# Reciprocal square roots on VectorE by a bit guess and Newton steps, in place of GpSimd's power, in a one-core encoder step

## The chip, the core and the metric

The kernel runs on one core of a Trainium2 chip. The metric is the device time of one execution in microseconds (us). The engines of the core are TensorE (PE, with its weight loads as PEld), VectorE (DVE), ScalarE (ACT), GpSimd (POOL) and SyncE (SP), whose queue issues nearly all DMA transfers. Each engine works through its own list of instructions in order; semaphores make one wait for another.

## The reference

One layer of a streaming encoder works on 1024 prompt tokens and 32 sample tokens with 1024 channels. The layer normalises its input, projects it to queries, keys, values and gates, runs three branches (windowed attention, a short convolution, attention into 256 memory tokens), gates and merges them, projects the result and adds the input; a last normalisation follows. What the change concerns is the normalisation, which occurs three times: of the input, of the memory tokens and of the output.

```python
def rmsnorm(x, g):
    x32 = x.astype(jnp.float32)
    y = x32 * lax.rsqrt(jnp.mean(x32 * x32, axis=-1, keepdims=True) + EPS)
    return (y * g.astype(jnp.float32)).astype(x.dtype)

# in reference(), cut:
q, k, v, ga, bb, cc, hh, gb, xq, gx, mg = split_inputs(xp, norm_g[l], w_in[l])   # rmsnorm(x, g) @ w
mk, mv = memory_kv(mem_prompt, mem_norm_g[l], w_mk[l], w_mv[l])                   # rmsnorm(mem, g) @ wk, wv
xp = xp + merge_branches(attn, ga, conv, bb, gb, xattn, gx, mg, w_pa[l], w_pb[l], w_px[l], w_out[l])
y_prompt = rmsnorm(xp, final_g)
y_sample = rmsnorm(xs, final_g)
```

## The kernel before

Channels lie on the partitions and tokens along the free axis; the 1056 tokens are held as two halves (the index `c`, 528 tokens each). Most products are done with numbers split into a high and a low part, three matmuls for one (`mm3`, L99 to L101), and the large input projections with a seven-product scheme on sums and differences of blocks. A framework puts the instructions of each engine into an order of its own before the program is built, from estimates of when operands are ready; so an edit in one function can move other instructions on the same engines, and on others.

The normalisation is done in these steps. ScalarE squares the eight pieces of a half (`x_squares`, L457) and VectorE adds the squares (`sq`, L461). `column_rstd` sums over the partitions with tiny matmuls against a column of ones (`cs...`, L417), so that tokens come to lie on partitions; VectorE scales the sum and adds epsilon (`va...`, L421); and GpSimd raises it to the power -0.5 (`rs...`, L424). `spread` (L428) multiplies the root with the identity on TensorE so that it stands along the free axis on all partitions (`rp...`), ScalarE copies that to `R...` (L436), and `x_norm` (L466) multiplies the eight pieces by it on VectorE. `x_blocks` and `x_sums` then split them into `xh` and `xl`.

At the start the first half has its root under the name `rsx` (88 partitions x 6 columns), the memory tokens theirs as `rsm` (128 x 2) and the second half again as `rsx`. Between them TensorE forms the memory keys `mkp` (`mk_step`, L585, four steps of eight products, each with 2 records in the trace). `mem_spread` (L557) spreads `rsm` to `rpm` and ScalarE copies it to `rm` (L563); `mk_out` multiplies `mkp` by `rm` (`mko`, L591) on VectorE, and the rest of it splits that into `mkh` and `mkl`. The first large products are those for keys and values (`pdkv`, `kv_group`), from the weights `whkv` and `wlkv`. The spreads and `pdkv` share two accumulation buffers (`bank2`), so the second `pdkv` waits until the copy has read the spread.

At the end `finish` (L1088) does the same for the output in four parts, under the name `rso` (88 x 3): two while output products (`wo`) for the second half of the tokens run, one a little later, and the last when nothing else is left.

Of the kernel before, what the change touches and what calls it, by code (L numbers as in the profile page):

```python
# [6 lines left out]
F32 = mybir.dt.float32  # L7
F32R = mybir.dt.float32r
AF = mybir.ActivationFunctionType
ALU = mybir.AluOpType  # L10
# [23 lines left out]
def stream_kernel(tc, A, O):  # L34
    nc = tc.nc
    act, dve, pool, pe, sp = nc.scalar, nc.vector, nc.gpsimd, nc.tensor, nc.sync

    from contextlib import ExitStack
    with ExitStack() as ctx:
        sb = ctx.enter_context(tc.tile_pool(name="sb", bufs=1))  # L40
        sm = ctx.enter_context(tc.tile_pool(name="sm", bufs=2))
# [28 lines left out]
        def bank2(name, i=None):  # L70

            if i is None:
                i = turns[0] = 1 - turns[0]
            return pp.tile([128, 2, 512], F32, name=name, tag=f"P{i}")

        def bank(name, shape=(128, 512)):
            return pq.tile(list(shape), F32, name=name, tag="Q")
# [13 lines left out]
        nhalf = cst[:, C_HALF:C_HALF + 1]  # L91
# [320 lines left out]
        def column_rstd(parts, cols, w, nm, pair_=False):  # L412

            ps = bank2(f"cs{nm}")[:, 0] if pair_ else bank(f"cs{nm}")
            for j in range(cols):
                for i, a in enumerate(parts):
                    pe.matmul(ps[:w, 2 * j:2 * j + 2], a[:, j * w:(j + 1) * w], one.broadcast_to([128, 2]),  # L417
                              start=i == 0, stop=i == len(parts) - 1)
            va = sm.tile([128, 6], F32, name=f"va{nm}", tag="va")
            pv_ = ps[:w, :2 * cols].rearrange("p (j t) -> p j t", t=2)  # L420
            dve.tensor_scalar(out=va[:w, :cols].unsqueeze(2), in0=pv_[:, :, 0:1], scalar1=1.0 / D, scalar2=EPS,  # L421
                              op0=ALU.mult, op1=ALU.add)
            rs = sm.tile([128, 6], F32, name=f"rs{nm}", tag="rs", bufs=3)
            pool.tensor_tensor(out=rs[:w, :cols], in0=va[:w, :cols], in1=nhalf[:w].broadcast_to([w, cols]), op=ALU.pow)  # L424
            return rs

        def spread(out, rs, j, w):
# [480 lines left out]
        for i in range(4):  # L908
            mem_scale(i)
            for k in (2 * i, 2 * i + 1):  # L910
                mv_step(k, wmv[k])
        sq = [x_squares(c) for c in range(2)]
        r0 = column_rstd([sq[0]], 6, 88, "x0", True)
        MS["rs"] = column_rstd([MS["acc"][:, :256], MS["acc"][:, 256:]], 2, 128, "m", True)
        mk_step(0)
        R0 = r_chunk(r0, "x0")
        x_norm(0, R0)
        mk_step(1)
        r1 = column_rstd([sq[1]], 6, 88, "x1", True)
        x_blocks(0, [xslot(slot(0, T4, l), f"b12{l}", F32R) for l in range(2)])  # L920
        kv = kv_group("kv", (T_K, T_V))
# [294 lines left out]
```

## Time and profile before

| what | value |
|---|---|
| median of 3 runs | 1005.92 us (1005.43 to 1006.57) |
| the profiled execution, its own time | 1011.11 us |
| its span, from the first to the last instruction | 1009.3 us |
| TensorE busy | 982.1 us, 97% of the span |
| VectorE busy | 510.7 us, 51%, 836 instructions |
| GpSimd busy | 561.4 us, 56%, 422 instructions |
| power operations on GpSimd (L424) | 7: two `rsx` (1.788 and 10.310 us), one `rsm` (1.023 us), four `rso` (0.852 to 1.296 us) |

Durations are taken from the one profiled execution, which is some 5 us longer than the median; a difference is carried over. An engine's idle time matters only where TensorE, the busiest, waits because of it.

### The profile page before, as it was taken

Reading aid. Unit: us, or ns where it says so; the run is one execution under the profiler, and the core shown is the slowest. Engines: PE = TensorE matmul, PEld = TensorE weight load, DVE = VectorE, ACT = ScalarE, POOL = GpSimd, SP = SyncE. Lnnn points to the kernel's source line nnn. Section 1 sums busy time; section 2 is a strip of 40 time slices with the busy share of each in tenths; the row PEclk is TensorE's granted clock in tenths of the full one; section 3 lists DMA queues with packets and bytes.
Section 4 is the critical chain, followed back from the end, with each engine's and each line's share of the span. In section 5 each row is a group of like instructions: output and inputs, shape, how many; then the busy total and the mean of one; then the engine's idle time right before and its main releaser. Section 6 shows DMA issues by size and latency. Waiting matters only on the chain.

```text
span 1009.3 us, 20193 instructions
## 1 busy us (share of the span) xinstructions
PE 982.1 (97%) x7887; PEld 958.1 (95%) x7887; DVE 510.7 (51%) x836; ACT 465.1 (46%) x969; POOL 561.4 (56%) x422
## 2 busy tenths in 40 slices
PE   8799999999999999999999999999999999999996
PEld 4699999999999999999999999999999999999996
DVE  3787333466575656565443333333374472552464
ACT  5454434455445454454454545545372242243452
POOL 0505677665667676767555555555554444444463
PEclk9899999999999999999999999999999999999998
DMA  9445633454423232322354444434686678653473
GB/s 338 145 150 156 204 133 110 152 170 138 128 67 103 74 112 85 99 75 86 105 161 149 154 151 148 138 120 153 210 281 201 182 201 254 183 188 88 126 233 118
DMA packets 115711, 153.06 MB, mean 152 GB/s; under 512 B 14400, under 2 KB 73888, under 8 KB 115616
## 3 DMA queue, kind: packets, MB, share of 16 engines
q1 hardware_dynamic: 115040, 151.24, 48.0%
q8 instruction: 62, 1.02, 0.4%
q10 hardware_dynamic: 576, 0.54, 0.2%
q14 instruction: 33, 0.27, 0.1%
HBM read 109.49 MB, written 42.25 MB: 150 GB/s over the span
## 4 chain that ended last, share of the span: by engine, by line
PE 85%; DVE 8%; DMA 2%; ACT 2%; POOL 2%; issue 1%; SPq 0%; POOLq 0%; DVEq 0%; ACTq 0%
PE y L99 4%; PE y L101 4%; PE y L100 4%; PE wo L99 3%; PE wo L101 3%; PE wo L100 3%; PE pamg L99 2%; PE pamg L100 2%; PE pdmg L99 2%; PE pamg L101 2%; PE pdmg L100 2%; PE pdmg L101 2%; PE pcmg L99 2%; PE pcmg L100 2%; PE pcmg L101 2%; PE mvp L550 2%
## 5 line engine op out<-in xcount | busy, mean ns | idle before, releaser
L95 POOL TENSOR_TENSOR wlp<-rp,whp 128x512 fp32r<-128x512 f32 x80 | 104.9, 1312 | 128.7 <-ACT whp L115 128.6
L115 ACT CAST whp<-rp 128x512 fp32r<-128x512 f32 x96 | 59.6, 621 | 130.3 <-PE y L100 78.7
L99 PE MATMUL y<-br,whp 128*128 128x264 f32 x384 | 109.2, 284 | 1.2 <-DVE z L271 1.2
L100 PE MATMUL y<-br,whp 128*128 128x264 f32 x384 | 109.1, 284 | 0.0
L101 PE MATMUL y<-br,wlp 128*128 128x264 f32 x384 | 109.0, 284 | 0.0
L95 POOL TENSOR_TENSOR wlmg<-S_mg,whmg 128x512 fp32r<-128x512 f32 x48 | 62.7, 1307 | 56.2 <-ACT whmg L115 42.5
L95 POOL TENSOR_TENSOR wlmg<-rmg,whmg 128x512 fp32r<-128x512 f32 x36 | 47.0, 1306 | 62.1 <-ACT whmg L115 59.3
L101 PE MATMUL wo<-zo,wlp 128*128 128x264 f32 x256 | 73.0, 285 | 0.8 <-POOL wlp L95 0.8
L99 PE MATMUL wo<-zo,whp 128*128 128x264 f32 x256 | 73.2, 286 | 0.3 <-ACT whp L115 0.3
L99 PEld LDWEIGHTS y<-br,whp 128*128 128x128 f32 x384 | 72.1, 188 | 1.3 <-ACT whp L115 1.3
L100 PE MATMUL wo<-zo,whp 128*128 128x264 f32 x256 | 72.6, 284 | 0.0
L100 PEld LDWEIGHTS y<-br,whp 128*128 128x128 f32 x384 | 72.3, 188 | 0.0
L101 PEld LDWEIGHTS y<-br,wlp 128*128 128x128 f32 x384 | 72.3, 188 | 0.0
L99 PE MATMUL pcmg<-xh,whmg 128*128 128x264 f32 x192 | 55.5, 289 | 1.2 <-DVE omg L218 1.2
L99 PE MATMUL pamg<-xh,whmg 128*128 128x264 f32 x192 | 55.3, 288 | 0.0
L99 PE MATMUL pdmg<-xh,whmg 128*128 128x264 f32 x192 | 55.2, 287 | 0.0
L100 PE MATMUL pcmg<-xl,whmg 128*128 128x264 f32 x192 | 54.7, 285 | 0.0
L100 PE MATMUL pdmg<-xl,whmg 128*128 128x264 f32 x192 | 54.7, 285 | 0.0
L100 PE MATMUL pamg<-xl,whmg 128*128 128x264 f32 x192 | 54.7, 285 | 0.0
L101 PE MATMUL pdmg<-xh,wlmg 128*128 128x264 f32 x192 | 54.6, 284 | 0.0
L101 PE MATMUL pcmg<-xh,wlmg 128*128 128x264 f32 x192 | 54.4, 284 | 0.0
L101 PE MATMUL pamg<-xh,wlmg 128*128 128x264 f32 x192 | 54.4, 283 | 0.0
(493 smaller groups left out, 3674.3 us busy)
## 6 DMA issues: line engine op xcount, KB each, us to landing
MGd<-omg SPq DMA_DIRECT2D x24, 528.0 KB, 3.6
sg<-MGd SPq DMA_DIRECT2D x48, 264.0 KB, 3.1
rmg<-in_w_in SPq DMA_DIRECT2D x48, 256.0 KB, 2.8
rp<-in_w_p SPq DMA_DIRECT2D x48, 256.0 KB, 3.1
rp<-in_w_out SPq DMA_DIRECT2D x48, 256.0 KB, 2.8
xr<-in_xT SPq DMA_DIRECT2D x8, 528.0 KB, 7.9
res<-in_xT SPq DMA_DIRECT2D x8, 528.0 KB, 5.7
qtw<-Qd SPq DMA_DIRECT2D x32, 128.0 KB, 2.6
```

Source lines behind the costliest of these rows:

```text
L95: eng.tensor_tensor(out=lo, in0=x, in1=hi.bitcast(F32), op=ALU.subtract)
L99: pe.matmul(out, lh, rh, start=first, stop=False, skip_group_check=free)
L100: pe.matmul(out, lh, rl, start=False, stop=False, skip_group_check=free)
L101: pe.matmul(out, ll, rh, start=False, stop=last, skip_group_check=free)
L115: act.copy(hi, src)
L550: pe.matmul(mps[m], mt(k)[:, m * 128:(m + 1) * 128], w, start=k == 0, stop=k == 7)
```

## The change

`column_rstd` computes the reciprocal square root on VectorE. The bits of the value `v` are read as an integer, shifted right by one, and subtracted from a constant, which gives a first guess `y` with the bits of a float; three Newton steps y <- y (1.5 - 0.5 v y y) follow. Each root is thus eleven instructions on VectorE, each working on the result of the one before, and GpSimd has no part in it. The function is called seven times: 77 instructions come and 7 go.

```diff
             rs = sm.tile([128, 6], F32, name=f"rs{nm}", tag="rs", bufs=3)
-            pool.tensor_tensor(out=rs[:w, :cols], in0=va[:w, :cols], in1=nhalf[:w].broadcast_to([w, cols]), op=ALU.pow)
+            t = sm.tile([128, 6], F32, name=f"rt{nm}", tag="rt", bufs=3)
+            v, y, t = va[:w, :cols], rs[:w, :cols], t[:w, :cols]
+            I32 = mybir.dt.int32
+            dve.tensor_scalar(out=t.bitcast(I32), in0=v.bitcast(I32), scalar1=1, scalar2=None, op0=ALU.logical_shift_right)
+            dve.tensor_scalar(out=y.bitcast(I32), in0=t.bitcast(I32), scalar1=-1.0, scalar2=float(0x5f3759df), op0=ALU.mult,
+                              op1=ALU.add)
+            for i in range(3):
+                dve.tensor_tensor(out=t, in0=y, in1=y, op=ALU.mult)
+                dve.scalar_tensor_tensor(out=t, in0=t, scalar=-0.5, in1=v, op0=ALU.mult, op1=ALU.mult)
+                dve.scalar_tensor_tensor(out=y, in0=t, scalar=1.5, in1=y, op0=ALU.add, op1=ALU.mult)
             return rs
```

The framework's order changes with it, in roughly the first tenth of the program and near its end; in between the order of every engine stays as it was. Lines behind the edit have numbers larger by nine in the changed kernel (L461 becomes L470, L585 becomes L594). In the new kernel L427 and L428 are the two integer instructions and L431 to L433 the Newton steps.

VectorE, from the first `vax` on, before (`sq` are the sums of squares of the second half, `xr` the input being normalised):

```order
L421 TENSOR_SCALAR vax_242<-csx_235 88x6
L421 TENSOR_SCALAR vam<-csm 128x2
L461 TENSOR_TENSOR sq_0_212<-sq_0_212,sq_2_217 128x528
L461 TENSOR_TENSOR sq_0_212<-sq_0_212,sq_3_220 128x528
L461 TENSOR_TENSOR sq_0_212<-sq_0_212,sq_4_223 128x528
L466 SCALAR_TENSOR_TENSOR xr_0_104<-xr_0_104,cst,Rx_271 128x528
L461 TENSOR_TENSOR sq_0_212<-sq_0_212,sq_5_226 128x528
L466 SCALAR_TENSOR_TENSOR xr_0_104<-xr_0_104,cst,Rx_271 128x528
```

The same place after the change:

```order
L421 TENSOR_SCALAR vax_242<-csx_235 88x6
L421 TENSOR_SCALAR vam<-csm 128x2
L427 TENSOR_SCALAR rtx_245<-vax_242 88x6
L470 TENSOR_TENSOR sq_0_212<-sq_0_212,sq_2_217 128x528
L428 TENSOR_SCALAR rsx_244<-rtx_245 88x6
L427 TENSOR_SCALAR rtm<-vam 128x2
L470 TENSOR_TENSOR sq_0_212<-sq_0_212,sq_3_220 128x528
L431 TENSOR_TENSOR rtx_245<-rsx_244 88x6
L428 TENSOR_SCALAR rsm<-rtm 128x2
L470 TENSOR_TENSOR sq_0_212<-sq_0_212,sq_4_223 128x528
L432 SCALAR_TENSOR_TENSOR rtx_245<-rtx_245,vax_242 88x6
L431 TENSOR_TENSOR rtm<-rsm 128x2
```

It goes on like this up to the addition of `sq_7`: all six additions now stand among the steps of the two chains, and the first multiplication of `xr` stands behind both chains.

VectorE at the second `rsx`, after the change (the last six steps of the chain; `xl` are low parts of the first half, `mko` and `mkl` the memory keys):

```order
L433 SCALAR_TENSOR_TENSOR rsx_320<-rtx_321,rsx_320 88x6
L95 TENSOR_TENSOR xl_5_340<-xr_2_114,xh_5_339 128x528
L431 TENSOR_TENSOR rtx_321<-rsx_320 88x6
L95 TENSOR_TENSOR xl_2_338<-xr_3_120,xh_2_337 128x528
L432 SCALAR_TENSOR_TENSOR rtx_321<-rtx_321,vax_318 88x6
L95 TENSOR_TENSOR xl_5_340<-xr_3_120,xh_5_339 128x528
L433 SCALAR_TENSOR_TENSOR rsx_320<-rtx_321,rsx_320 88x6
L600 TENSOR_TENSOR mko_396<-mkp_277,rm 128x512
L431 TENSOR_TENSOR rtx_321<-rsx_320 88x6
L600 TENSOR_TENSOR mko_405<-mkp_357,rm 128x512
L432 SCALAR_TENSOR_TENSOR rtx_321<-rtx_321,vax_318 88x6
L95 TENSOR_TENSOR mkl_400<-mko_396,mkh_399 128x512
```

One row follows that belongs to the chain, its last step (L433). Before the change `mko` stood behind the normalisation of the second half, well after this place.

TensorE at the end of `mkp`, before:

```order
L585 MATMUL mkp_324<-memt_116,rmk_150 128x256 x2
L428 MATMUL rpx_341<-cst,rsx_298 128x88 x6
L428 MATMUL rpm<-cst,rsm 128x128 x2
L99 MATMUL pdkv_407<-xh_0_302,whkv_383 128x264
L100 MATMUL pdkv_407<-xl_0_303,whkv_383 128x264
```

And after the change:

```order
L594 MATMUL mkp_357<-memt_116,rmk_150 128x256 x2
L437 MATMUL rpm<-cst,rsm 128x128 x2
L99 MATMUL pdkv_490<-xh_0_335,whkv_428 128x264
L100 MATMUL pdkv_490<-xl_0_336,whkv_428 128x264
L437 MATMUL rpx_374<-cst,rsx_320 128x88 x6
L99 MATMUL pdkv_440<-xh_0_335,whkv_416 128x264
```

The spread of the memory root and two products for the values now stand ahead of the spread of the second half's root. Further up, the first eight products of `mkp` (16 records) have moved ahead of the first spread. At the very end of the program the eleven instructions of the last `rso` stand in a row on VectorE, with nothing between them.

## Rows read from the trace of the kernel before

**Rows 1.** Page, first part: busy us, share of the span, instructions

```profile
PE 982.1 (97%) x7887; PEld 958.1 (95%) x7887; DVE 510.7 (51%) x836; ACT 465.1 (46%) x969; POOL 561.4 (56%) x422
```

**Rows 2.** Stretches: length, busy us (instructions) of each engine, granted clock, DMA

```profile
core 0: us, PE busy (x) PEld busy (x) DVE busy (x) ACT busy (x) POOL busy (x), PEclk, DMA share, GB/s
...
45.00:48.95 3.95, 0.00 (x0) 0.00 (x0) 2.76 (x5) 1.25 (x2) 3.94 (x1) 0.89 0.79 256
48.95:54.75 5.80, 5.76 (x26) 5.70 (x27) 2.23 (x4) 2.54 (x5) 0.00 (x0) 0.50 0.01 2
```

**Rows 3.** Waits of TensorE: us in total, times, longest

```profile
PE rpx L428 <- POOL rsx L424: 6.1, 2, 4.0
...
PE rpo L428 <- POOL rso L424: 1.2, 1, 1.2
```

**Rows 4.** Timeline at the first root: start, length (us), engine, line

```profile
24.86 0.16 DVE L421 TENSOR_SCALAR vax<-csx 88x6 f32<-88x6 f32 x1 [2.33 <-PE csx L417]
24.94 0.15 DVE L421 TENSOR_SCALAR vam<-csm 128x2 f32<-128x2 f32 x1
25.00 2.32 DVE L461 TENSOR_TENSOR sq<-sq,sq 128x528 f32<-128x528 f32 x3
25.10 1.79 POOL L424 TENSOR_TENSOR rsx<-vax,cst 88x6 f32<-88x6 f32 x1 [24.66 <-DVE vam L421]
...
26.94 2.25 PE L428 MATMUL rpx<-cst,rsx 88*128 88x88 f32 x12 [2.12 <-POOL rsx L424]
```

**Rows 5.** Timeline at the second root

```profile
37.84 7.15 PE L585 MATMUL mkp<-memt,rmk 128*128 128x256 f32 x32
...
38.62 10.31 POOL L424 TENSOR_TENSOR rsx<-vax,cst 88x6 f32<-88x6 f32 x1 [10.74 <-DVE vax L421]
...
39.70 2.55 DVE L95 TENSOR_TENSOR xl<-xr,xh 128x528 fp32r<-128x528 f32 x4
...
48.99 2.86 PE L428 MATMUL rpx<-cst,rsx 88*128 88x88 f32 x12 [4.00 <-POOL rsx L424]
...
51.64 1.13 PE L428 MATMUL rpm<-cst,rsm 128*128 128x128 f32 x4
51.88 0.60 ACT L436 COPY Rx<-rpx 128x528 f32<-128x528 f32 x1 [5.32 <-PE rpx L428]
52.52 5.52 DVE L466 SCALAR_TENSOR_TENSOR xr<-xr,cst,Rx 128x528 f32<-128x528 f32 x8 [4.76 <-ACT Rx L436]
...
52.54 0.59 PE L99 MATMUL pdkv<-xh,whkv 128*128 128x264 f32 x1
...
52.80 0.37 ACT L563 COPY rm<-rpm 128x256 f32<-128x256 f32 x1 [0.32 <-PE rpm L428]
```

**Rows 6.** Instructions on tile `mko`: ns min/median/max, first and last start

```profile
L591 DVE TENSOR_TENSOR mko<-mkp,rm x2: 677/678/680, 58.0 to 58.6; 128x512 f32<-128x512 f32 x2
```

**Rows 7.** Timeline: small VectorE operations elsewhere

```profile
341.27 0.21 DVE L303 SCALAR_TENSOR_TENSOR och<-cw,och 128x2 f32<-128x2 f32 x1
...
692.79 0.67 DVE L633 TENSOR_REDUCE mxxs<-Sxs 32x2 f32<-32x512 f32 x1
693.50 0.55 DVE L634 TENSOR_SCALAR mxxs<-mxxs 32x2 f32<-32x2 f32 x1
```

**Rows 8.** Tile `rmk`: its transfers, ns at the queue, us to landing

```profile
L49 SPq DMA_DIRECT2D rmk<-in_w_mk x8: 328/328/328, 17.2 to 24.5; - x8
...
DMA to landing us min/median/max: 5.4/7.7/8.0
```

**Rows 9.** Timeline at the last root

```profile
999.91 0.16 DVE L421 TENSOR_SCALAR vao<-cso 88x3 f32<-88x3 f32 x1 [1.56 <-PE cso L417]
1000.15 0.85 POOL L424 TENSOR_TENSOR rso<-vao,cst 88x3 f32<-88x3 f32 x1 [6.84 <-DVE vao L421]
...
1001.05 1.58 PE L428 MATMUL rpo<-cst,rso 88*128 88x88 f32 x6 [1.25 <-POOL rso L424]
```

**Rows 10.** Timeline at the first two output roots

```profile
954.37 1.29 POOL L95 TENSOR_TENSOR wlp<-rp,whp 128x512 fp32r<-128x512 f32 x1 [0.68 <-ACT whp L115]
...
957.95 0.80 PE L428 MATMUL rpo<-cst,rso 88*128 88x88 f32 x6
```

## The prediction

> **What bounds the kernel now.** I read the engine totals of the page first: TensorE is busy 97% of the span and VectorE 51% [rows 1], so time can only be won where TensorE stands still. The table by stretches names one such place: from 45.0 to 48.95 us it does nothing at all [rows 2]. Then I read whom TensorE waited for: 6.1 us, in two waits, for GpSimd's reciprocal roots of the start (`rsx`, L424) and 1.2 us for the last one (`rso`) [rows 3]. These 7.3 us are all that seven power operations cost TensorE directly. The timeline then shows each of the three places.
>
> At the first root VectorE forms `vax` at 24.86, GpSimd raises to a power from 25.10 to 26.89, and TensorE starts spreading the result at 26.94 [rows 4]. At the second, GpSimd's operation of the same shape takes 10.31 us instead of 1.79, and TensorE starts the spread at 48.99, 4.00 us after it ran out of work [rows 4, 5]. VectorE was busy through most of it; the operation on GpSimd is tiny, so what stretches it is VectorE's work beside it. At the last root, `vao` ends at 1000.07, the power takes 0.85 us and the spread starts at 1001.05: 0.98 us from one to the other [rows 9]. Nothing is left there to hide it.
>
> **The first root gets later.** The power goes, and eleven dependent VectorE operations take its place, two of integers and bits and three times three for Newton. In VectorE's new order six wide additions of squares (`sq`) stand between the steps, and the two-column chain for `rsm` as well. The wide additions, which also depend on each other, cost 2.32 us for three, so (2.32 - 0.71) / 2 = 0.81 from start to start [rows 4]. The chain begins behind `vax` at 25.0. With a first step of 0.2 and the six additions the last one starts at 25.2 + 5 x 0.81 = 29.3 and ends at 30.0; the trios of small steps between them add 0.1. Four steps of the x chain are then left, of which the first can start as the addition ends.
>
> What does a small step cost? No row has this chain. A lone small operation takes 0.15 to 0.21 us and a second, independent one starts 0.08 behind the first [rows 4, 7]. A dependent one starts 0.04 us after the end of its forerunner behind a reduction (692.79 + 0.67 to 693.50) and 0.1 after the wide additions [rows 4, 7]. So 0.16 + 0.04 = 0.20 is the lower end; the upper end is 0.59, from the dependent small operation that took 0.55 us and the same 0.04 [rows 7]. That one ran while GpSimd worked, which at the start and at the very end it doesn't, so I take 0.24, near the lower end. Four steps are 1.0 us, and the root is ready at about 31.0, where it was 26.89: 4.1 us later (bounds: 30.7 at 0.20 and 32.5 at 0.59).
>
> [...]
>
> **What covers that.** TensorE's order moves the first 8 product steps of `mkp` (16 records) ahead of the first spread. They need the weights `rmk`, the first issued at 17.2 and landed within 8.0 us, at 25.2 [rows 8]. So TensorE has work from 25.2 to about 29 while VectorE makes the root, and this work is gone later: 16 of the 32 records that take 7.15 us, 3.6 us [rows 5]. From the start of the first spread (26.94) to the end of the last `mkp` record (37.84 + 7.15 = 45.0) it took 18.05 us; now 18.05 - 3.6 = 14.5, from 31.0 to 45.5.
>
> **The second root is not earlier.** This is where the obvious gain of 8 us or so goes. VectorE gets the first `Rx` at 31.0 + 2.25 + 0.7 = 34.0, norms eight pieces (5.52 us) [rows 5] and reaches `vax` of the second half at 39.5; it could finish eleven steps by 42.5. But its new order puts one wide operation between every two steps, and in front of the ninth and tenth step it places the two `mko` products and in front of the last the first `mkl`. `mko` needs `rm`, which needs the spread `rpm`, which TensorE does only after the last `mkp` record, at 45.5. VectorE runs its queue in order, so the root waits for a thing that it doesn't need. `rpm` takes about 0.6 us (1.13 at half the clock) and the copy `rm` 0.37 with two hand-overs [rows 5]: 46.5. Then `mko` 0.68, a step, `mko` 0.68, a step, `mkl` (0.69, as `mko`) and the last step [rows 6]; the small steps between cost their 0.08 overlap: 2.25 us, and the root is ready at 48.75, against 48.93. The bounds follow the first root's: 48.45 to 50.3.
>
> Then the spread, 2.86 us as before at the half clock, and the copy `Rx` 0.60 with hand-overs of 0.08, which frees the bank for the first `pdkv` product [rows 5]. It starts at 48.8 + 2.86 + 0.7 = 52.35, against 52.54: 0.2 us won. Two `pdkv` products already stand ahead of the wait: 0.2 to 0.4 us. [...] After the idle of 2.12 us before 26.94 the same spread took 2.25 us instead of 2.86 [rows 4, 5], so part of the slow stretch may go: 0 to 1.1 us, taken 0.4. The start as a whole: **-1.0 us**, from -2.2 to +1.5.
>
> From there on VectorE has as many wide operations as before up to the next weights that TensorE needs (51 in either order), and the order of every engine is the same in the middle, so I cost it at nothing. If that cover fails, TensorE waits for VectorE at the second pass over `pdkv`, where I see some 0.3 us of slack at most.
>
> **The last root.** Eleven steps with nothing between them: 11 x 0.24 = 2.6 us where GpSimd took 0.98. Nothing hides it: **+1.6 us**, from 11 x 0.20 - 0.98 = +1.2 to 11 x 0.59 - 0.98 = +5.5; I keep +2.9 as the working upper end (0.35 a step), since 0.59 is a row with GpSimd at work. The three roots before it lie under `wo` products. There two chains run with 22 steps from about 952.3, beside GpSimd's 1.29 us `wlp`, and the spread stands at 957.95 on TensorE [rows 10]: 22 x 0.12 to 0.24 is 2.6 to 5.3 us, so they are ready between 955 and 957.6, or some later if `wlp` holds VectorE once: 0 to +0.8, taken 0.
>
> **Sum.** The profiled execution has a span of 1009.3 us and took 1011.11, while the median of the runs shown is 1005.92; I carry differences over. -1.0 + 1.6 + 0 = +0.6: 1011.7 for an execution that is profiled, **1006.5 us** for the median. About 0.2%, 2.0 us, is what a measurement of this kernel can tell from no change.
>
> **Rivals.** (1) *Small dependent steps are dear*, place: the tail, and the first root. At 0.35 us a step the tail costs 11 x 0.35 - 0.98 = +2.9, and the 19 steps before the first spread add 19 x 0.1 = +1.9, so the start turns from -1.0 to +0.9: +3.8, **1009.7 us**. It decides from some 0.28 a step, where the sum passes +2.0. For it: the row at 0.55; against it: that row had GpSimd beside it. [...]
> (2) *`rm` is no hindrance*: if `mkp` ends earlier, VectorE goes on through `mko` at its own pace, at 39.5 + 8 x (0.62 + 0.1) = 45.3 by the four `xl` in 2.55 us [rows 5], and the second root comes at 47.5, not 48.75. The start then wins 1.3 more and most of the slow clock, -3.0, and with the lower tail, +1.2, it is -1.8 to -2.6: **1003.5 us**. Against it: TensorE's records set 45.5 unless the first root comes before 30.
> (3) *The change doesn't do what it says where it matters*: the ten-microsecond power was cheap since other work hid most of it, and roots ready earlier change nothing at all, while the tail alone counts: +1.6 with no gain at the start, **1007.5**. That is inside my range and within "same".
>
> **How the numbers follow.** The forecast, within 2.0 us of before, has 0.5 and rival 3 0.16 on the same side: same 0.66. Rival 1 with its neighbours has 0.24, with 0.02 for a mishap of the order, so slower 0.26. Rival 2 has 0.08: faster 0.08. The likeliest case alone spans 1004.9 to 1008.4 (-2.2 + 1.2 and, at its upper, +0.9 + 1.6). For 8 in 10 the range takes in rival 1 as priced and the middle of rival 2's side: 1004.2 to 1009.7.
>
> **What would show it.** Right: `rsx` of the second half ends at 48 to 49.5 with an `mko` that waited for ACT's `rm` in front of its last steps; the first spread starts near 31; GpSimd is idle until its first weight sums; in the tail some 2.6 us pass between `vao` and the spread. Wrong: a second spread before 47.5, steps above 0.28 us from start to start, or TensorE waiting for `rpo` near 958. A gain of over 2 us would mean that the in-order argument on `mko` failed.

## The result: 11 us slower, and what the profile after shows

| what | before | changed |
|---|---|---|
| median of 4 runs each | 1005.67 us (1005.11 to 1006.57) | 1016.85 us (1014.08 to 1018.28) |
| ratio | | 1.0104, 95% interval 1.0072 to 1.0137 |
| the profiled execution, its span | 1011.11 us, 1009.3 us | 1016.62 us, 1014.8 us |
| nine more runs beside 14 of before, on one chip, later | 1005.26 us | 1016.84 us (1013.29 to 1020.14), ratio 1.0097 (1.0066 to 1.0128) |

The forecast was 1006.5 us with a range up to 1009.7. The change is slower, outside that range. Note the third line: the two profiled executions are only 5.5 us apart, while the medians are 11.2 apart. So the two traces by themselves can't explain the loss: half of it is missing from them.

Page of the changed kernel, first part (busy us, share of the span, instructions); it answers to [rows 1]:

```profile
PE 985.7 (97%) x7887; PEld 960.1 (95%) x7887; DVE 519.2 (51%) x913; ACT 465.6 (46%) x969; POOL 541.2 (53%) x415
```

The 77 new instructions are there on VectorE, and the seven powers are gone from GpSimd. The waits of TensorE in the changed kernel (us in total, times, longest), against [rows 3]:

```profile
PE rpo L437 <- DVE rso L433: 4.1, 2, 2.5
PE rpx L437 <- DVE rtm L431: 2.4, 1, 2.4
...
PE rpx L437 <- DVE rsx L433: 1.7, 1, 1.7
```

Before it waited 7.3 us for GpSimd's roots, now 8.2 us for VectorE's, and 4.1 of these are at two output roots, where it had been one.

**The second root of the start** went almost as the prediction said. The timeline of the changed kernel (start, length, engine, line, and in brackets the idle time before and what ended it), against [rows 5]:

```profile
39.15 7.15 PE L594 MATMUL mkp<-memt,rmk 128*128 128x256 f32 x32
39.36 0.15 DVE L421 TENSOR_SCALAR vax<-csx 88x6 f32<-88x6 f32 x1
...
44.90 0.15 DVE L433 SCALAR_TENSOR_TENSOR rsx<-rtx,rsx 88x6 f32<-88x6 f32 x1
...
46.78 0.37 ACT L572 COPY rm<-rpm 128x256 f32<-128x256 f32 x1 [6.15 <-PE rpm L437]
47.19 0.69 DVE L600 TENSOR_TENSOR mko<-mkp,rm 128x512 f32<-128x512 f32 x1 [2.14 <-ACT rm L572]
...
49.17 0.15 DVE L433 SCALAR_TENSOR_TENSOR rsx<-rtx,rsx 88x6 f32<-88x6 f32 x1
...
49.38 1.92 PE L437 MATMUL rpx<-cst,rsx 88*128 88x88 f32 x12 [1.66 <-DVE rsx L433]
```

Eight of the eleven steps are done at 45.05. Then VectorE stands still for 2.14 us in front of `mko`, which waits for `rm`, with three steps of the root queued behind it. The root is ready at 49.32, where GpSimd's had been ready at 48.93.

**The third output root** is where these two traces differ. Timeline of the changed kernel:

```profile
982.59 0.16 DVE L431 TENSOR_TENSOR rto<-rso 88x3 f32<-88x3 f32 x1
982.75 1.27 POOL L95 TENSOR_TENSOR wlp<-rp,whp 128x512 fp32r<-128x512 f32 x1 [2.33 <-DVE rto L431]
982.78 1.26 DVE L432 SCALAR_TENSOR_TENSOR rto<-rto,vao 88x3 f32<-88x3 f32 x1
984.07 0.16 DVE L433 SCALAR_TENSOR_TENSOR rso<-rto,rso 88x3 f32<-88x3 f32 x1
...
984.88 0.15 DVE L433 SCALAR_TENSOR_TENSOR rso<-rto,rso 88x3 f32<-88x3 f32 x1
...
985.17 1.06 PE L437 MATMUL rpo<-cst,rso 88*128 88x88 f32 x6 [1.61 <-DVE rso L433]
```

GpSimd begins to split a weight at 982.75; the Newton step that starts 0.03 us later takes 1.26 us instead of 0.16, as long as the split. The root is late and TensorE stands still for 1.61 us. The hold is 1.1 us of that; the rest is the length of the chain and the wide operations of VectorE between its steps. The stretches behind the wait show what follows (length, busy us and instructions of each engine, granted clock, DMA):

```profile
982.00:986.00 4.00, 2.39 (x20) 2.21 (x18) 3.71 (x12) 2.18 (x4) 1.27 (x1) 0.96 0.60 189
986.00:990.00 4.00, 4.00 (x23) 4.00 (x23) 2.09 (x5) 1.00 (x2) 2.67 (x4) 0.61 0.63 187
990.00:996.00 6.00, 6.00 (x52) 6.00 (x51) 2.94 (x6) 3.73 (x7) 2.49 (x3) 1.00 0.48 150
```

After the idle time the granted clock is 0.61 of full speed for four microseconds (0.50 from 986.0 to 989.0 us), and 23 matmuls are done where the next stretch has 52 in six, some 35 in four. Why the Newton step was as long as GpSimd's split beside it, 1.26 and 1.27 us, isn't shown.

**The last root**, against [rows 9]:

```profile
1004.20 0.16 DVE L421 TENSOR_SCALAR vao<-cso 88x3 f32<-88x3 f32 x1 [1.49 <-PE cso L417]
...
1006.33 0.16 DVE L433 SCALAR_TENSOR_TENSOR rso<-rto,rso 88x3 f32<-88x3 f32 x1
...
1006.63 1.55 PE L437 MATMUL rpo<-cst,rso 88*128 88x88 f32 x6 [2.47 <-DVE rso L433]
```

From `vao` to the spread 2.43 us pass instead of 1.14: 1.3 us more. Eleven steps lie 0.193 us apart.

### The profile page after: what moved, and what is told of

It is laid out like the page before. It is cut to its first block, busy times and chain, and to the rows that moved or that the text cites. A ratio compares the mean times of both kernels' runs of the same rounds, so it can differ in the third digit from the quotient of the medians.

```text
span 1014.8 us, 20257 instructions
## 1 busy us (share of the span) xinstructions
PE 985.7 (97%) x7887; PEld 960.1 (95%) x7887; DVE 519.2 (51%) x913; ACT 465.6 (46%) x969; POOL 541.2 (53%) x415
## 4 chain that ended last, share of the span: by engine, by line
PE 89%; DVE 5%; issue 2%; DMA 2%; ACT 1%; POOL 0%; SPq 0%; POOLq 0%; ACTq 0%; DVEq 0%
PE y L99 4%; PE y L101 4%; PE y L100 4%; PE wo L101 3%; PE wo L99 3%; PE wo L100 3%; PE pamg L99 2%; PE pamg L100 2%; PE pdmg L99 2%; PE pamg L101 2%; PE pdmg L100 2%; PE pdmg L101 2%; PE pcmg L99 2%; PE pcmg L100 2%; PE pcmg L101 2%
```

## The experiments

### A second trace of before, and the change in parts

The first question was where the missing 5.4 us are. Four kernels ran together: the kernel before again; and the Newton steps in some of the roots alone, with the power on GpSimd in the others. The edit for the start alone (for the output roots alone, and the third output root alone, the condition is `nm[0] != "o"` and `nm != "o10"`):

```diff
             rs = sm.tile([128, 6], F32, name=f"rs{nm}", tag="rs", bufs=3)
+            if nm[0] == "o":
+                pool.tensor_tensor(out=rs[:w, :cols], in0=va[:w, :cols], in1=nhalf[:w].broadcast_to([w, cols]), op=ALU.pow)
+                return rs
             t = sm.tile([128, 6], F32, name=f"rt{nm}", tag="rt", bufs=3)
```

Before, again: 

> The kernel before, unchanged, for a second trace beside its times. The two traces at hand, of before and of the changed kernel, differ by 5.5 us (1011.11 and 1016.62), the medians by 11.2 us, so the first trace of before is of an execution about 5.4 us longer than the usual one. Theory A (the extra 5.4 us of that execution lie in the stretch of the output products, where TensorE already waited for `rp` loads and `wlp` between 958 and 975 us): time 1005.1 to 1006.6, the first `wo` product at 898 us as before, and the end about 5 us earlier. Rival B (they lie at the start, in the loads before the first product of the projections): the whole trace after 60 us about 5 us earlier, with the same steps. If the trace is again at 1011, the tracing itself is what adds, and the traces of the two kernels can't be set side by side to better than 5 us.

Start alone: 

> The Newton steps for the roots of the inputs and of the memory alone; the four output roots take the power on GpSimd again. Theory A (the loss lies at the output roots; the start is about even, last pdkv 77.2 us against 76.6 in the traces): 1005 to 1007, ratio 1.000 within 0.002. Rival B (the traces hide the loss because the traced execution of before had a slow start; the start costs about 5 us): 1010 to 1012. Rival C (the start gains about 1 us, as predicted, and only the output roots lose): 1004 to 1005.5.

Output roots alone: 

> The Newton steps for the four output roots alone; the three roots of the start take the power on GpSimd again. Theory A (the third output root, behind GpSimd's `wlp`, and the half clock after it, and the last root carry the loss): 1011 to 1017, that is 5.5 us to the whole 11 us over the kernel before. Rival B (the start carries half): about 1010 to 1011. Rival C (each output root costs only its own steps, 11 x 0.19 against 0.85 to 1.3 us, and only the last is on the path): 1007.

Third output root alone: 

> The Newton steps for the third output root alone (the first part of the second row half); all other roots take the power. Theory A (in the trace its chain is held 1.26 us by a step that runs beside GpSimd's `wlp`, TensorE is idle 1.6 us and then runs at a granted clock of 0.50 for three us): 1009 to 1014, at least 4 us of the loss. Rival (the loss is spread over all output roots, about the same for each): 1006.5 to 1008.

Measured: before again 1006.77 us (1003.07 to 1011.36, 12 runs; 35 runs of before beside it: 1004.99, 1003.21 to 1013.0); start alone 1011.07 (1008.13 to 1013.72), ratio 1.0040 (1.0016 to 1.0064); output roots alone 1013.11 (1007.79 to 1018.93), ratio 1.0063 (1.0033 to 1.0092); third output root alone 1006.51 (1005.25 to 1012.28), ratio 1.0001 (0.9975 to 1.0027).

Both theories of the first expectation were wrong: the new trace of before is again long, at 1011.36. Tracing isn't what adds: in the list four other executions lie at 1010.26 to 1011.26 and seven at 1003.07 to 1007.78, and a later trace is of one at 1004.65. What the list shows instead is that **the kernel before has two times**. Over the whole study 123 of its executions were timed: 83 at 1002.8 to 1007.8 us (median 1004.6) and 40 at 1009.7 to 1014.5 (median 1011.2), and none between 1007.8 and 1009.7. (The chip doesn't decide it: both groups occur on each of the three chips that timed the kernel most, mixed from one execution to the next, and the next runs show the instruction that makes them.) The first trace of before was of the upper group, and its median of the lower.

So the parts must be read against a group. The start alone lost 6 us against the lower group and nothing against the upper: rival B of its expectation. The output roots alone are a mixture, 1007.79 at the lowest and 1018.93 at the highest, since their start is that of before. The third output root alone is 2 us above the lower group, where I had expected 4 and more, so that theory was wrong on the size; its `wo` products take 102.4 us in the trace, 3.4 more than before. And that trace, at 1006.43, gave the clue to the groups: its second power took 1.72 us, not 10.31.

### The two durations of one power

Two later traces of before, one of each group, show it in the same program. The execution at 1004.65 us (start, length, line, idle time before):

```profile
26.57 1.57 PE L428 MATMUL rpx<-cst,rsx 88*128 88x88 f32 x12 [2.12 <-POOL rsx L424]
...
37.75 0.16 DVE L421 TENSOR_SCALAR vax<-csx 88x6 f32<-88x6 f32 x1 [0.32 <-PE csx L417]
37.83 0.69 DVE L95 TENSOR_TENSOR xl<-xr,xh 128x528 fp32r<-128x528 f32 x1
37.99 1.71 POOL L424 TENSOR_TENSOR rsx<-vax,cst 88x6 f32<-88x6 f32 x1 [10.47 <-DVE vax L421]
...
44.49 1.47 PE L428 MATMUL rpx<-cst,rsx 88*128 88x88 f32 x12
```

Here TensorE comes to the second spread at 44.49, and the root has been ready since 39.70. The execution at 1010.04 us:

```profile
26.36 2.14 PE L428 MATMUL rpx<-cst,rsx 88*128 88x88 f32 x12 [2.12 <-POOL rsx L424]
...
37.08 0.70 DVE L95 TENSOR_TENSOR b<-xr,b 128x528 fp32r<-128x528 f32 x1
37.70 0.15 DVE L421 TENSOR_SCALAR vax<-csx 88x6 f32<-88x6 f32 x1
37.77 0.69 DVE L95 TENSOR_TENSOR xl<-xr,xh 128x528 fp32r<-128x528 f32 x1
37.93 10.30 POOL L424 TENSOR_TENSOR rsx<-vax,cst 88x6 f32<-88x6 f32 x1 [10.63 <-DVE vax L421]
```

The operation is the same, and so is its order against VectorE's; GpSimd starts 0.23 to 0.24 us behind the start of `vax` in both. The difference is ahead of `vax`: in the first, VectorE had waited 0.32 us for `csx`; in the second it came straight from `b`. In these two it goes back to the first spread `rpx`, 11 us earlier: at the full clock it takes 1.57 us, and where the clock falls while it runs, 2.14. The granted clock in the stretch from 26.3 to 28.0 us (third number from the end) was 1.00 and 0.76:

```profile
26.30:28.00 1.70, 1.43 (x13) 1.43 (x13) 0.66 (x1) 0.00 (x0) 1.22 (x2) 1.00 1.05 387
...
26.30:28.00 1.70, 1.64 (x11) 1.65 (x12) 0.44 (x1) 0.00 (x0) 1.00 (x2) 0.76 1.06 390
```

VectorE gets its `Rx` that much later (28.18 and 28.53) and reaches `vax` without waiting. In three other traces of before the first spread took 2.03 to 2.25 us, and in the remaining one, at 1011.36, it ran at the full clock but a microsecond late; all four have the same end: no idle time, 10.31 us. What came first in this chain is read from traces; only the idle time ahead of `vax` was forced, below.

> The kernel before, unchanged, for a trace of the lower group. If the execution is at 1003 to 1006.9 us: power 1.7 to 1.8 us, keys and values end near 70 us; at 1009.6 or more: 10.31 us and 76.6 to 77.9 us. An execution near 1004 with a long power would refute that the two groups are the power's two durations.

Five traces of before were taken besides the first one; the one at 1004.65 us had the short power, those at 1011.36, 1010.74, 1011.18 and 1010.04 the long one. What it is worth can be read on the products `pdkv` and `wo` (tile views: count, ns min/median/max, first and last start). The execution of before at 1004.65 us, then the changed kernel:

```profile
L99 PE MATMUL pdkv<-xh,whkv x48: 281/283/396, 46.6 to 69.7; 128*128 128x264 f32 x48
...
L99 PE MATMUL wo<-zo,whp x256: 280/285/392, 891.7 to 990.9; 128*128 128x264 f32 x128
```

```profile
L99 PE MATMUL pdkv<-xh,whkv x48: 281/283/586, 47.2 to 77.2; 128*128 128x264 f32 x48
...
L99 PE MATMUL wo<-zo,whp x256: 280/285/567, 898.6 to 1001.7; 128*128 128x264 f32 x128
```

This is the whole account of these two executions, 1002.8 and 1014.8 us of span, 12.0 us apart: 6.9 us until the first `wo` product (7.5 at the end of `pdkv`, of which 0.6 come back), 3.9 us among the `wo` products (99.2 us long before, 103.1 now), and 1.2 us from there to the end (11.9 and 13.1). The 7.5 us at `pdkv` are a later start, 51.99 us (behind two products done before) instead of 46.6, and the lower clock behind TensorE's wait; in the changed kernel:

```profile
52.00:57.20 5.20, 5.20 (x23) 5.20 (x24) 5.20 (x8) 3.85 (x7) 0.00 (x0) 0.50 0.99 304
```

### Forcing the power either way

If idle time ahead of `vax` lets GpSimd in, then the order alone must be able to force either duration. In the first kernel the splits of the first half stand behind `vax` on VectorE, so it waits there; in the second `vax` stands behind all of them.

```diff
-            dve.tensor_scalar(out=va[:w, :cols].unsqueeze(2), in0=pv_[:, :, 0:1], scalar1=1.0 / D, scalar2=EPS,
+            VA[nm] = dve.tensor_scalar(out=va[:w, :cols].unsqueeze(2), in0=pv_[:, :, 0:1], scalar1=1.0 / D, scalar2=EPS,
...
-        x_blocks(0, [xslot(slot(0, T4, l), f"b12{l}", F32R) for l in range(2)])
+        with tc.issue_after(VA["x1"].ins):
+            x_blocks(0, [xslot(slot(0, T4, l), f"b12{l}", F32R) for l in range(2)])
```

```diff
+        x_blocks(0, [xslot(slot(0, T4, l), f"b12{l}", F32R) for l in range(2)])
         r1 = column_rstd([sq[1]], 6, 88, "x1", True)
-        x_blocks(0, [xslot(slot(0, T4, l), f"b12{l}", F32R) for l in range(2)])
```

Idle time ahead: 

> The kernel before, with the power on GpSimd; the sums and splits of the first half (`x_blocks(0)`) are ordered behind the second root's `vax` on VectorE, so that VectorE comes to `vax` early and has to wait there for `csx`. In the traces so far the second power took 10.31 us three times, when VectorE came to `vax` without idle time, and 1.72 us once, when VectorE had waited 0.32 us for `csx` just ahead of it; the times of before fall in two groups to match, 1003.2 to 1006.4 and 1009.8 to 1013.0 us (23 and 12 of 35). Theory A (idle time ahead of `vax` lets GpSimd in): every execution in the lower group, 1003 to 1006.5 us, power 1.7 to 1.8 us in the trace, ratio 0.997 to 0.999. Rival B (which of the two it is has nothing to do with that wait): both groups again, in about the same shares. Rival C (the wait itself costs as much as it wins): one group at 1006 to 1008.

No idle time: 

> The kernel before; the second root's `vax` now stands behind all eight splits of the first half on VectorE, so that `csx` is long there and VectorE has no idle time ahead of it. It comes some 4 us later, at about 43 us. Theory A (without idle time ahead of `vax` GpSimd gets in only when VectorE runs out of work, at about 47.8 us): the power lasts 5 to 6 us to about 49 us, every execution in the upper group, 1009.5 to 1013 us. Rival B (chance decides each time): two groups, and in the lower one the root is ready by about 45 us, at 1004 to 1006 us.

Measured without idle time: 1010.09 us (1009.15 to 1012.28), all 12 executions in one group, as theory A said. In its trace the power takes 6.60 us, until VectorE has run out of work:

```profile
41.51 0.15 DVE L421 TENSOR_SCALAR vax<-csx 88x6 f32<-88x6 f32 x1
...
41.74 6.60 POOL L424 TENSOR_TENSOR rsx<-vax,cst 88x6 f32<-88x6 f32 x1 [14.35 <-DVE vax L421]
```

With idle time: 1008.97 us (1006.02 to 1013.74). The power is short in the trace (1.71 us, behind 1.55 us of idle time) and `pdkv` ends at 70.2, but the time is not that of the lower group: theory A was right on the power and wrong on the time. A new wait took most of the gain: VectorE, now behind, splits the weights of the next products late, and behind that wait the granted clock is 0.61 from 86 to 90 us.

```profile
PE pdq L101 <- DVE wlq L95: 3.0, 1, 3.0
```

That wait is 0.5 us in the traces of before at 1004.65, 1010.04 and 1011.11. Two of the twelve executions, at 1012.89 and 1013.74, lie 4 us above the others; whether GpSimd was kept out there in spite of the idle time wasn't traced and stays open. In the kernel with both edits below, which has 0.94 us of idle time there in its trace, none of eleven did.

### The Newton steps at the start, and their place in the order

The second root alone with Newton steps (condition `nm != "x1"`), and the changed kernel with the memory keys written later:

```diff
+        next(kv)
         mem_spread()
         mk_out()
-        next(kv)
         mv_out()
```

Second root alone: 

> The Newton steps for the second root of the start alone; the first roots and the output roots take the power. In this order the eleven steps stand between the splits and ahead of `mko`, so the root is ready at about 47 us, against 49.3 us with all start roots changed, and against 39.8 or 48.9 us with the power. Theory A (the time of the second root sets the start, the first roots cost nothing): 1006 to 1009 us, in one group, without the times near 1004 of the power. Rival B (the first roots, spread 4.8 us later, are what costs): 1004 to 1005. Rival C (the second root costs the whole 7 us wherever its steps stand): 1010 to 1012.

Memory keys later: 

> The changed kernel, with the spreading of the memory root and the scaling of the memory keys (`rpm`, `rm`, `mko`) written behind the first block of keys and values, so that VectorE does all eleven steps of the second root before it comes to `mko`. Theory A (VectorE stood 2.14 us before `mko` for `rm`, with three steps of the root behind it, which made the root late): root ready at about 47 us instead of 49.33, time 1011.5 to 1014 against 1016.85, so 3 to 5 us of the loss are this place in the order; the rest of the loss stays. Rival B (what waits at the start is something else, such as the split weights `wlkv`): 1015 to 1018.

Measured: the second root alone 1008.16 us (1006.09 to 1010.75), one group, ratio 1.0018 (0.9999 to 1.0036), as theory A. In its trace, which is of its slowest execution, the last step ends at 46.83, `pdkv` at 71.6, and TensorE waits 2.7 us for `wlq`. So by the medians the second root by Newton, with what follows from it, is 3 us cheaper than the long power and 3.5 dearer than the short one. The start with all its roots changed lost 6: the other 3 us come with the first roots, whether by their own lateness or by the place of the second root's last steps behind `mko`, and these two weren't told apart.

With the memory keys later the last step ended at 46.20, as expected, the last `pdkv` products ran at 70.8 instead of 77.4, and yet the time was 1016.45 us (1011.38 to 1017.52): theory A was right on the root and wrong on the time, which is rival B's. The traced execution, at 1011.38, is the fastest of the six; it shows again the wait that comes in place of the root:

```profile
PE pdq L101 <- DVE wlq L95: 3.0, 2, 1.8
```

In that execution the earlier root is worth something, but less than the 6.6 us by which `pdkv` ends earlier: the first `wo` product comes at 895.6 instead of 898.6, since TensorE then waits for `wlq` at 85.9 and 88.8 us. VectorE has no idle time above 0.2 us from the second normalisation, at 50.55 us, until then, so it can't be earlier with `wlq`. That most executions of this kernel lose 5 to 6 us against its own trace isn't explained by one trace; it stays open.

### The output roots without the start's two groups

The kernel that always keeps GpSimd waiting at the second root has one group of times, so it is a steady ground for the end. On it the four output roots get the Newton steps; in the second kernel the third output root is also spread one product later:

```diff
-            if n in (9, 11, 17, 18):
+            if n in (9, 11, 17, 19):
```

Newton steps at the output roots: 

> The kernel that always keeps GpSimd waiting at the second root (median 1010.09, 1009.15 to 1012.28: one group), with the Newton steps at the four output roots: what these cost, without the start's two groups mixed in. Theory A (third output root 2.2 to 4.1 us by the traces, last root 1.3 us, the first two nothing): 1013.5 to 1015.5. Rival B (only the last root lies on the path): 1011 to 1012. Rival C (the first two output roots cost as well): 1016 to 1018.

Third root spread later: 

> The kernel of the run beside it (always waiting at the second root, Newton steps at the output roots), with the third output root spread one output product later, 4.2 us, so that its eleven steps are over when TensorE comes to it. Theory A (the third root costs because TensorE comes to `rpo` 1.6 us before its last step; nothing else there is late): TensorE waits for DVE `rso` only at the last root, 1011 to 1012.5. Rival B (the later normalisation of that part then collides with the last products' `wlp` on VectorE and GpSimd): 1013 or more.

Measured: 1013.83 us (five of six at 1013.52 to 1014.35, one at 1020.59) and 1012.31 us (1010.80 to 1014.50, 5 runs), against 1010.09 on the same ground with the power, which was timed on another chip. Both are as theory A. With five and six executions the medians price the third root only roughly: the two traces are already 2.5 us apart at the first `wo` product, ahead of the place where the kernels differ. The waits of TensorE from 890 us on, and the last products, of the first kernel and of the second:

```profile
PE rpo L440 <- DVE rso L434: 4.1, 2, 2.5
...
L99 PE MATMUL wo<-zo,whp x256: 281/285/391, 898.8 to 999.9; 128*128 128x264 f32 x128
```

```profile
PE rpo L440 <- DVE rso L434: 2.5, 1, 2.5
...
L99 PE MATMUL wo<-zo,whp x256: 281/285/390, 896.3 to 995.6; 128*128 128x264 f32 x128
```

With the spread one product later the 1.6 us wait is gone, and the `wo` products take 99.3 us, as with the power (98.8 to 99.3 in eleven traces), instead of 101.1. Six traces have the Newton steps at this root in its old place: 101.1, 101.2, 101.2, 102.4, 103.1 and 105.2 us. The wait is 1.6 us each time, and each time a step of the chain was held, for 1.17 to 1.26 us. In the three traces of 101.1 and 101.2 us the granted clock stays at 1.00 behind it; in those of 102.4, 103.1 and 105.2 us it falls for some 3 us: 0.50 from 986 to 989 us in that of 103.1 and from 988 to 990 in that of 105.2, and in that of 102.4 matmuls of 0.42 us instead of 0.29 from 977.92 to 980.56. So the price of this wait is 2 us, or some 3.5 where the clock falls. What goes beyond that is a wait for a weight ahead of the root, which is 0.3 us in the first trace of before, 0.8 in that of 103.1 us and 1.4 in that of 105.2 us, where the clock fell behind it too (matmuls of 0.42 us instead of 0.28 from 973.98 to 976.84, and granted 0.86 from 976 to 980 us):

```profile
972.30 0.39 PE L99 MATMUL wo<-zo,whp 128*128 128x264 f32 x1 [1.43 <-ACT whp L115]
```

What decides whether the clock falls wasn't tried.

### Two kernels put together from this

Power kept, with one split ahead of `vax` and the others behind it, and the four weights of `q_direct` split at once:

```diff
-            for i in range(2):
-                w = [w_pair(raw_load(A["w_in"][2 * (T_Q + t + i) + h], f"r{nm}{i}{h}"), f"{nm}{i}{h}", dve)
-                     for h in range(2)]
+            ws = [[w_pair(raw_load(A["w_in"][2 * (T_Q + t + i) + h], f"r{nm}{i}{h}"), f"{nm}{i}{h}", dve)
+                   for h in range(2)] for i in range(2)]
+            for i in range(2):
+                w = ws[i]
...
+                        if c == 0 and (kh, kk, s) != (0, 0, 0):
+                            with tc.issue_after(VA["x1"].ins):
+                                put(ops[kh, s], kk, xb(c, kh, s, kk))
...
```

> The kernel before with the power, and two edits of the order at the start: on VectorE the splits of the first half from the second on stand behind the second root's `vax` (only the first stands ahead of it), so that VectorE waits some 0.3 to 0.9 us for `csx` there; and the four weights of `q_direct` are split at once, so that the last two `wlq` no longer stand behind the last sums of the second half. In the run with all splits behind `vax` the power took 1.71 us, keys and values ended at 70.2 us instead of 76.9, and TensorE then lost 3.0 us at 85 us waiting for `wlq`, and part of the clock behind that. Theory A (with `wlq` early the gain stays): one group, 1003 to 1005.5 us, no execution above 1008, ratio 0.997 to 0.999. Rival B (another split of VectorE's, such as `xl`, is late in place of `wlq`): 1005.5 to 1009. Rival C (the wait ahead of `vax` doesn't decide how long the power takes): some executions at 1009 and above.

Measured: **1002.61 us** (1001.76 to 1005.61, 11 runs), before beside it 1004.76, ratio 0.9974 (0.9954 to 0.9993): one group, as theory A said, its median 0.4 us under that theory's range. It is 0.3% faster than before with its two groups, and 2 us under the median of the lower one. The trace (1002.59) has the idle time and the short power, and no wait for `wlq` at all:

```profile
37.94 0.16 DVE L424 TENSOR_SCALAR vax<-csx 88x6 f32<-88x6 f32 x1 [0.94 <-PE csx L420]
...
38.18 1.72 POOL L427 TENSOR_TENSOR rsx<-vax,cst 88x6 f32<-88x6 f32 x1 [10.47 <-DVE vax L424]
```

The same kind of mending for the Newton kernel: memory keys later, the four weights split at once, the third output root spread later.

> The changed kernel with all its Newton steps, and three edits of the order: `rpm`, `rm` and `mko` behind the first block of keys and values (as in the run that gave 1016.45 us), the four weights of `q_direct` split at once, and the third output root spread one output product later. Theory A (of the 12 us over the kernel before's usual time, 2 to 3 are the place of the second root's last steps, 3 are `wlq`, 2 to 4 the third output root; 1.3 at the last root and some 2 us of the longer chain at the start stay): 1007.5 to 1010.5. Rival B (each mended wait is only replaced by the next): 1012 or more.

Measured: 1008.35 us (1005.77 to 1009.99, 11 runs), ratio 1.0019 (0.9996 to 1.0042), theory A. Three edits of the order, none of them in the root itself, together take back 8.5 of the 12 us; they weren't priced one by one. What is left in its trace is the last root (13 us from the last `wo` product to the end, against 11 to 12), and at the start 1.9 us of TensorE's idle time at the first spread, and 1.5 us at `pdq` for another of VectorE's pieces (`q1q`).

### The changed kernel, again

> The changed kernel, unchanged, for more executions. Theory A (start 7 us over the lower group of before, third output root 2.2 to 4.1, last root 1.3): 1014 to 1018 us, median 1015 to 1017, no execution under 1012.5, ratio to before 1.009 to 1.013. Rival (the first four were high by chance and the parts were over-counted): median under 1013.

Measured: 1016.84 us (1013.29 to 1020.14, 9 runs), ratio 1.0097 (1.0066 to 1.0128), with the first four runs 13 executions from 1013.29 to 1020.14. The median is as theory A, but three of the nine lie above its 1018. The parts add up near the median: 1004.6, the lower group, + 7 + 2 to 3.5 + 1.3 = 1015 to 1016.5. The traced execution, at 1018.01, has the longer wait for a weight, shown above, on top; what the two at 1019.71 and 1020.14 have wasn't traced.

## Why the prediction was wrong

**The step that failed first is in the sum: "I carry differences over."** The profiled execution, at 1011.11, was 5.2 us above the median, and I took that for a constant that both kernels share. It was the very operation that the change removes: a power of 10.31 us, which most executions don't have. Against the trace the start came out at about nothing, inside its bounds (-1.0 forecast; +0.6 at the end of `pdkv`, +0.2 at the first `wo` product); against the executions that make the median it costs 7 us. The rows to see it by were all there: 1.79 us and 10.31 us for one operation on one engine [rows 4, 5], 3.95 us of idle time and 5.80 us at half the clock behind it [rows 2], and a span 5 us longer than the times. I explained the 10.31 us by VectorE's work beside it and didn't ask whether it happens every time.

**The second step is "three roots before it lie under `wo` products ... taken 0", up to +0.8.** For the first two that holds: a step of theirs was held by a `wlp` as well, for 1.25 us, but the roots were ready and the spread came at 958.17, without a wait, against 957.95. For the third it doesn't: some 2 us, and 3.5 where the clock fell. I worked the sum out for the place with rows [rows 10] and let the third root go with it. Even the mechanism was in the text ("if `wlp` holds VectorE once"), priced at one hold, without TensorE's idle time and the clock behind it. And no run shows the 0.4 us that the sum takes off at the start for a shorter slow stretch: in the changed kernel TensorE idled 1.66 us ahead of the second spread, the spread took 1.92 us instead of 2.86, and the granted clock was then 0.50 from 51.0 to 57.2 us, where it had been 0.50 from 48.95 to 54.75.

**What held.** Against the traced execution the second root isn't earlier, since `mko` stands in front of the last steps and waits for `rm`: forecast ready at 48.75, measured 49.32, with all that precedes it 0.9 us late in that trace (`vax` of the first half at 25.79 instead of 24.86). Against the usual execution, where it was ready at 39.70, it is nearly 10 us later. The first spread came at 31.71; forecast 31.0, and with the same 0.9 us it agrees. `pdkv` at its place was forecast for 52.35 and came at 51.99. The last root, +1.6 forecast, cost +1.3: a dependent step is 0.193 us from start to start where 0.24 was taken.

**The rivals.** Dear small steps (1009.7 us) came nearest to the time but not for its reason: the steps were cheap. The rival that `rm` is no hindrance didn't come true: VectorE stood 2.14 us for it. Where the order forced it, with the keys later, the root came at 46.20, but the gain of that rival didn't follow in the median, and in the trace TensorE waited for `wlq` instead. The prediction had set the work of VectorE up to the next weights at nothing and named "the second pass over `pdkv`" as the place where that would show; it showed one stage later, at `pdq`. The third rival, that the long power was cheap, is refuted: executions with the short one are 6.6 us faster.

## What to carry to other kernels

When the profiled execution's time isn't near the median, it isn't an offset to carry over: find the operation that is long in it, and price the change against the executions without it. An operation that takes six times its usual length beside another engine can be one that doesn't always do so, as here, and a few more traces of the kernel before tell how often; the cheap cure can be the order (here 0.94 us of idle time in the right place), not another engine. And the chain of tiny dependent instructions was cheap by itself, 0.19 us a step; what it cost was where it stood, in a queue behind something that waits, or beside an engine that can hold one of its steps for a microsecond (1.17 to 1.26 us instead of 0.16).

## What the hardware showed that I had not expected

One GpSimd instruction of 88x6 elements took 1.71 to 1.72 us or 10.30 to 10.31 us beside the same queue of wide VectorE operations. In the short case nothing on VectorE is slower for it: its splits keep their 0.62 us from start to start. In the long case GpSimd got on only when VectorE ran dry: fifteen operations later, at 47.76 in the first trace of before, and the power ended at 48.93; with `vax` later, at 47.16 and 48.34, that is 1.2 us after it both times. The wide operations there lie 0.62 us apart and last 0.69 to 0.70, so each has begun before the last one ends; that this is what keeps GpSimd out is a guess. In the short case the power began 0.16 us behind a wide operation of VectorE that lasts 0.69 us (`xl` at 37.83, the power at 37.99), and took 1.71 us beside it. What all traces show, and both orders that were forced, is that idle time on VectorE just ahead of the instruction that releases GpSimd goes with the short power. Why isn't shown.

The first idle time of TensorE at the start is 2.12 us in every trace of before, but the clock falls at a different point of the spread behind it (granted 1.00 or 0.76 from 26.3 to 28.0 us), and that half microsecond decided, in the two traces set side by side above, between times 6.6 us apart by the medians.
